# A small load that nothing reads, in front of the first load of a rotary embedding kernel

## The chip, the cores and the metric

The kernel runs on one core of one Trainium2 chip. The metric is the device time of one execution in microseconds (us), the median of several runs. The kernel before takes 316.29 us (three runs, 316.23 to 316.83).

## What is computed

A rotary position embedding with interleaved pairs. `x` has the shape (8, 2048, 16, 64): batch, position, head, head dimension, in fp32. `cos` and `sin` have the shape (2048, 32). The reference, cut to what matters:

```python
x_pairs = x.reshape(batch, seq_len, num_heads, head_dim // 2, 2)
x1, x2 = x_pairs[..., 0], x_pairs[..., 1]
out1 = x1 * cos - x2 * sin
out2 = x1 * sin + x2 * cos
out = np.stack([out1, out2], axis=-1).reshape(batch, seq_len, num_heads, head_dim)
```

`x` is 67.1 MB and so is the output.

## The kernel before

**Tiling.** The 2048 positions of a batch are spread over 128 partitions, 16 rows (`K`) to each. A row is 16 heads of 64 numbers, 1024 fp32 or 4 KB, so one partition's share of a batch is one piece of 64 KB in the DRAM. In SBUF a batch is kept in bf16. The buffer `xt` has five places for a batch; `HOME` gives the place of each of the eight batches, so that batches 5, 6 and 7 come to where 0, 1 and 2 were. GpSimd's DMAs turn fp32 into bf16 on the way in and back on the way out (`load`, L68 to L70, and `store`, L72 to L74).

**The head.** The first 4 rows of batch 0 go another way, so that work can start early: SyncE (SP) loads them in fp32 (L101) into the buffer `head`, which shares its place with the scratch buffer `qt`, and ScalarE (ACT) casts them into `xt` (L108). Meanwhile GpSimd (POOL) issues, on its own queue and in this order: sin (L102), cos (L103), rows 4 to 15 of batch 0 (L104), batches 1 and 2 in one DMA, batches 3 and 4 in one DMA (both L70).

**The work.** VectorE (DVE) makes two tables from sin and cos (L110 to L112) and then calls `rotate` for the 4 rows, the other 12 rows, and each of the seven other batches. A `rotate` is three operations over all its rows: the product with the sin table into `qt` (L89), the product with the cos table in place (L92), and the sum with the pairs of `qt` swapped (L97).

**The order.** It is written out by hand under `tc.manual_schedule()`; each engine works its own queue in the order of the lines, and waits between engines are put in where data are shared. The store of batch 0 is held back until DVE has come to batch 2, by two tiny copies on ACT (L120, L121). A tiny copy on POOL that reads the end of batch 4 (`mark`, L126) stands ahead of the store of batches 1 and 2. Batches 5, then 6 and 7, are loaded when the places that they come to have been stored. The last batch leaves in another way: ACT casts it to fp32 in four parts into places 3 and 4 of `xt` (`wide`, L138), and SP stores it (L139). SP has only these two DMAs, L101 and L139.

**Buffers.** The pool `consts` holds `xt`, the tables, and the two single numbers `gate` and `mark`; the pool `stage` behind it holds the one buffer that `head` and `qt` share.

Of the kernel before, what the change touches and what calls it, by code (L numbers as in the profile page):

```python
# [2 lines left out]

# [4 lines left out]


@with_exitstack  # L10
def kernel(
    ctx: ExitStack,
    tc: tile.TileContext,
    x: bass.AP,
    cos: bass.AP,
    sin: bass.AP,
    out: bass.AP,
):
    nc = tc.nc
    fp32 = mybir.dt.float32  # L20
    bf16 = mybir.dt.bfloat16
    mult = mybir.AluOpType.mult
    add = mybir.AluOpType.add

    B, S, H, D = x.shape
    P = 128
    K = S // P
    KP = 16
    D2 = D // 2
    HD = H * D  # L30
    NX = 5
    HEAD = 4
    PART = 4
    STAGE = 3


    HOME = [0, 1, 2, 3, 4, 0, 1, 2]

    x_t = x.rearrange("b (p k) h d -> b p k (h d)", p=P, k=K)
    out_t = out.rearrange("b (p k) h d -> b p k (h d)", p=P, k=K)  # L40
    x_r = x.rearrange("b (p k) h d -> p b (k h d)", p=P, k=K)
    out_r = out.rearrange("b (p k) h d -> p b (k h d)", p=P, k=K)
    cos_t = cos.rearrange("(p k) c -> p (k c)", p=P, k=K)
    sin_t = sin.rearrange("(p k) c -> p (k c)", p=P, k=K)

    consts = ctx.enter_context(tc.tile_pool(name="consts", bufs=1))
    stage = ctx.enter_context(tc.tile_pool(name="stage", bufs=1))

    xt = consts.tile([P, NX, K * HD], bf16)
    cos_sb = consts.tile([P, K * D2], fp32)  # L50
    sin_sb = consts.tile([P, K * D2], fp32)
    c_tab = consts.tile([P, K, D], bf16)
    s_tab = consts.tile([P, K, D], bf16)

    wide = (
        xt[:, STAGE : STAGE + 2]
        .rearrange("p a c -> p (a c)")
        .bitcast(fp32)
        .rearrange("p (k c) -> p k c", c=HD)
    )  # L60

    gate = consts.tile([1, 1], bf16)
    mark = consts.tile([1, 1], bf16)

    def home(b, k0=0, k1=K):
        return xt[:, HOME[b], k0 * HD : k1 * HD].rearrange("p (k c) -> p k c", c=HD)

    def load(b, n):  # L68
        h = HOME[b]
        nc.gpsimd.dma_start(out=xt[:, h : h + n], in_=x_r[:, b : b + n])  # L70

    def store(b, n):  # L72
        h = HOME[b]
        nc.gpsimd.dma_start(out=out_r[:, b : b + n], in_=xt[:, h : h + n])  # L74

    def rotate(b, k0=0, k1=K, between=None):
        nk = k1 - k0
        xp = home(b, k0, k1)
        qt = stage.tile([P, KP, HD], bf16, name="qt", tag="work")

        def rows(a):
            return a.rearrange("p k (h e) -> p k h e", h=H, e=D)

        def tab(a):
            return dataclasses.replace(
                a, offset=a.offset + k0 * D, ap=[a.ap[0], [D, nk], [0, H], [1, D]]
            )

        nc.vector.tensor_tensor(out=rows(qt[:, :nk]), in0=rows(xp), in1=tab(s_tab), op=mult)  # L89
        if between is not None:  # L90
            between(qt)
        nc.vector.tensor_tensor(out=rows(xp), in0=rows(xp), in1=tab(c_tab), op=mult)  # L92
        q_swap = dataclasses.replace(
            qt, offset=qt.offset + 1, ap=[qt.ap[0], [2, nk * HD // 2], [-1, 2]]
        )
        x3 = xp.rearrange("p k (a j) -> p (k a) j", j=2)
        nc.vector.tensor_tensor(out=x3, in0=x3, in1=q_swap, op=add)  # L97

    with tc.manual_schedule():
        head = stage.tile([P, HEAD, HD], fp32, name="st", tag="work")  # L100
        nc.sync.dma_start(out=head[:, :HEAD], in_=x_t[0, :, :HEAD])  # L101
        nc.gpsimd.dma_start(out=sin_sb, in_=sin_t)  # L102
        nc.gpsimd.dma_start(out=cos_sb, in_=cos_t)  # L103
        nc.gpsimd.dma_start(out=home(0, HEAD), in_=x_t[0, :, HEAD:])  # L104
        load(1, 2)
        load(3, 2)

        nc.scalar.copy(out=home(0, 0, HEAD), in_=head[:, :HEAD])  # L108
        s2 = s_tab.rearrange("p k (i j) -> p (k i) j", j=2)
        nc.vector.tensor_copy(out=s2[:, :, 0], in_=sin_sb)  # L110
        nc.vector.tensor_scalar_mul(s2[:, :, 1], sin_sb, -1.0)  # L111
        nc.vector.tensor_copy(  # L112
            out=c_tab.rearrange("p k (i j) -> p (k i) j", j=2),
            in_=cos_sb.to_broadcast([P, K * D2, 2]),
        )
        rotate(0, 0, HEAD)
        rotate(0, HEAD, K)

        def first_store(qt):
            nc.scalar.copy(out=gate, in_=qt[:1, KP - 1, HD - 1 :])  # L120
            nc.scalar.copy(out=xt[:1, HOME[0], :1], in_=xt[:1, HOME[0], :1])  # L121
            store(0, 1)

        rotate(1)
        rotate(2, between=first_store)
        nc.gpsimd.tensor_copy(out=mark, in_=xt[:1, 4, K * HD - 1 :])  # L126
        store(1, 2)
        load(5, 1)
        load(6, 2)
        rotate(3)  # L130
        rotate(4)
        store(3, 2)
        for b in range(5, B):
            rotate(b)
            if b == 6:
                store(5, 2)
        for k in range(0, K, PART):
            nc.scalar.copy(out=wide[:, k : k + PART], in_=home(B - 1, k, k + PART))  # L138
        nc.sync.dma_start(out=out_t[B - 1], in_=wide)  # L139


# [1 line left out]
_INS = ['x', 'cos', 'sin']  # L143
_OUTS = [((8, 2048, 16, 64), 'float32')]


# [23 lines left out]
```

## Time and profile before

| what | value |
|---|---|
| time, median of three runs | 316.29 us (316.23 to 316.83) |
| time of the profiled execution | 316.21 us |
| span of the profiled execution, first to last instruction | 314.4 us |
| DVE busy | 210.4 us, 67% of the span, 30 instructions |
| ACT busy, POOL busy | 19.3 us (6%), 12.4 us (4%) |
| DMA queue q0, issued by POOL | 91.75 MB, counted as written, 92.0% of 16 engines' span |
| DMA queue q1, issued by SP | 10.49 MB, counted as written, 7.9% |
| head (L101): 2048 KB, from issue to landing | 8.0 us |
| sin (L102), cos (L103): 256 KB each | 7.6 and 7.4 us |
| rows 4 to 15 of batch 0 (L104): 3072 KB in bf16 | 21.2 us |

The span runs from the first to the last instruction of the profile; the profiled execution's own time holds 1.8 us more around it. A line such as `L101 SPq` is an instruction by which SP's queue issues a DMA: its length is the time of the issue, not of the transfer. The busy share of the DMA is the mean over the core's 16 DMA engines, on which all queues run. A DMA is cut into packets, which the trace records one by one with their starts, lengths and sizes.

### The profile page before, as it was taken

To read this page: it belongs to the slowest core of one execution; us is meant where nothing else is said; L and a number is where in the kernel's file an instruction comes from. 1 tells how busy PE (TensorE), PEld (TensorE's weight loads), DVE (VectorE), ACT (ScalarE), POOL (GpSimd) and SP (SyncE) were. 2 spreads that over 40 slices of the span, in tenths; PEclk is the share of its full clock that TensorE was granted. 3 is DMA by queue.
4 is the path that set the end of the run, shared out by engine and by line. 5 is a ranking of instruction groups with operands and counts; after the bars stand their busy time and mean duration, and the time that the engine had idled before them with its cause. 6 is when DMAs were issued, how large, how long until landed. Compare 5 with 4: busy or idle time off the path is not lost.

```text
span 314.4 us, 114 instructions
## 1 busy us (share of the span) xinstructions
DVE 210.4 (67%) x30; ACT 19.3 (6%) x8; POOL 12.4 (4%) x16
## 2 busy tenths in 40 slices
DVE  0549950099999999999992299903999999200000
ACT  1400000000000000000000000000000000790000
POOL 4000000000002500000000000000000000000000
DMA  7999999999999999999999999999999999999996
GB/s 296 238 267 200 200 200 267 200 200 217 250 200 267 459 475 400 400 492 442 400 200 246 221 200 200 250 217 333 400 525 409 400 400 525 409 400 400 525 409 267
DMA packets 2512, 102.24 MB, mean 325 GB/s; under 512 B 208, under 2 KB 208, under 8 KB 336
## 3 DMA queue, kind: packets, MB, share of 16 engines
q0 software_dynamic: 2224, 91.75, 92.0%
q1 hardware_dynamic: 288, 10.49, 7.9%
HBM read 67.63 MB, written 67.11 MB: 429 GB/s over the span
## 4 chain that ended last, share of the span: by engine, by line
DVE 64%; another core or an unknown queue 13%; DMA 7%; ACT 3%; ACTq 1%; issue 0%; POOL 0%; DVEq 0%; PEldq 0%
DVE qt L89 21%; DVE xt L92 21%; DVE xt L97 21%; DMA xt<-in_x_dram 7%; ACT xt L138 3%; ACTq L165 1%; POOL sin_sb L102 0%; POOL cos_sb L103 0%; DVEq L89 0%; DVEq L92 0%; PEldq L165 0%
## 5 line engine op out<-in xcount | busy, mean ns | idle before, releaser
L89 DVE TENSOR_TENSOR qt<-xt,s_tab 128x16384 bf16<-128x16384 bf16 (+2 forms) x9 | 69.7, 7744 | 49.3 <-DMA xt<-in_x_dram 47.0
L92 DVE TENSOR_TENSOR xt<-xt,c_tab 128x16384 bf16<-128x16384 bf16 (+2 forms) x9 | 69.7, 7743 | 0.4
L97 DVE TENSOR_TENSOR xt<-xt,qt 128x16384 bf16<-128x16384 bf16 (+2 forms) x9 | 69.7, 7744 | 0.3
L138 ACT CAST xt<-xt 128x4096 f32<-128x4096 bf16 x4 | 14.1, 3600 | 171.7 <-DVE xt L97 171.7
L74 POOL DMA_DIRECT2D out_dram<-xt x4 | 2.7, 672 | 184.9 <-ACT xt L121 93.5
L110 DVE CAST s_tab<-sin_sb 128x512 bf16<-128x512 f32 x1 | 0.5, 456 | 8.9 <-DMA sin_sb<-in_sin_dram 8.9
L120 ACT COPY gate<-qt 1x1 bf16<-1x1 bf16 x1 | 0.2, 194 | 85.1 <-DVE qt L89 85.1
L126 POOL COPY mark<-xt 1x1 bf16<-1x1 bf16 x1 | 5.0, 5040 | 2.6 <-DMA xt<-in_x_dram 2.6
L70 POOL DMA_DIRECT2D xt<-in_x_dram x4 | 2.7, 694 | 43.2 <-DMA out_dram<-xt 43.2
L108 ACT CAST xt<-st 128x4096 bf16<-128x4096 f32 x1 | 3.6, 3605 | 6.7 <-DMA st<-in_x_dram 6.7
L108 ACT ACT_TABLE_LOAD x1 | 1.3, 1283 | 0.7 <-PEq L154 0.7
L102 POOL DMA_DIRECT2D sin_sb<-in_sin_dram x1 | 0.7, 696 | 0.8 <-PEq L165 0.8
L112 DVE CAST c_tab<-cos_sb 128x1024 bf16<-128x1024 f32 x1 | 0.7, 685 | 0.0
L103 POOL DMA_DIRECT2D cos_sb<-in_cos_dram x1 | 0.6, 569 | 0.0
L104 POOL DMA_DIRECT2D xt<-in_x_dram x1 | 0.6, 557 | 0.0
L111 DVE TENSOR_SCALAR s_tab<-sin_sb 128x512 bf16<-128x512 f32 x1 | 0.4, 445 | 0.0
L121 ACT COPY xt<-xt 1x1 bf16<-1x1 bf16 x1 | 0.2, 188 | 0.0
L154 POOL MEMSET const-float32-0.0<- 128x1 f32 x1 | 0.1, 99 | 0.2 <-issue 0.2
L154 POOL MEMSET const-bfloat16-1.0<- 128x1 bf16 x1 | 0.1, 103 | 0.0
L154 POOL MEMSET const-float32-1.0<- 128x1 f32 x1 | 0.1, 99 | 0.0
L154 POOL MEMSET const-uint8-127<- 128x1 uint8 x1 | 0.1, 99 | 0.0
## 6 DMA issues: line engine op xcount, KB each, us to landing
xt<-in_x_dram POOLq DMA_DIRECT2D x3, 8192.0 KB, 59.4
xt<-in_x_dram POOLq DMA_DIRECT2D x1, 4096.0 KB, 57.6
xt<-in_x_dram POOLq DMA_DIRECT2D x1, 3072.0 KB, 21.2
st<-in_x_dram SPq DMA_DIRECT2D x1, 2048.0 KB, 8.0
sin_sb<-in_sin_dram POOLq DMA_DIRECT2D x1, 256.0 KB, 7.6
cos_sb<-in_cos_dram POOLq DMA_DIRECT2D x1, 256.0 KB, 7.4
out_dram<-xt POOLq DMA_DIRECT2D x4, 49.8
out_dram<-xt SPq DMA_DIRECT2D x1, 30.0
```

The costliest lines, as they stand in the source:

```text
L70: nc.gpsimd.dma_start(out=xt[:, h : h + n], in_=x_r[:, b : b + n])
L74: nc.gpsimd.dma_start(out=out_r[:, b : b + n], in_=xt[:, h : h + n])
L89: nc.vector.tensor_tensor(out=rows(qt[:, :nk]), in0=rows(xp), in1=tab(s_tab), op=mult)
L92: nc.vector.tensor_tensor(out=rows(xp), in0=rows(xp), in1=tab(c_tab), op=mult)
L97: nc.vector.tensor_tensor(out=x3, in0=x3, in1=q_swap, op=add)
L102: nc.gpsimd.dma_start(out=sin_sb, in_=sin_t)
L103: nc.gpsimd.dma_start(out=cos_sb, in_=cos_t)
L108: nc.scalar.copy(out=home(0, 0, HEAD), in_=head[:, :HEAD])
L112: nc.vector.tensor_copy(out=c_tab.rearrange("p k (i j) -> p (k i) j", j=2), in_=cos_sb.to_broadcast([P, K * D2, 2]),)
L126: nc.gpsimd.tensor_copy(out=mark, in_=xt[:1, 4, K * HD - 1 :])
L138: nc.scalar.copy(out=wide[:, k : k + PART], in_=home(B - 1, k, k + PART))
L165: with _tile.TileContext(nc) as tc:
```

## The change

A buffer of 32 partitions by 128 fp32 is added to `consts`, behind `gate` and `mark`. Ahead of the head's load, SP loads into it the first 128 numbers (512 bytes) of the first row of every fourth partition's share of batch 0: 32 pieces of 512 bytes, 16 KB, 256 KB apart in the DRAM. These bytes are part of what the head's load reads, too. Nothing reads the buffer.

```diff
     gate = consts.tile([1, 1], bf16)
     mark = consts.tile([1, 1], bf16)
+    touch = consts.tile([32, 128], fp32)
...
     with tc.manual_schedule():
         head = stage.tile([P, HEAD, HD], fp32, name="st", tag="work")
+        nc.sync.dma_start(out=touch, in_=x_t[0, ::4, 0, :128])
         nc.sync.dma_start(out=head[:, :HEAD], in_=x_t[0, :, :HEAD])
         nc.gpsimd.dma_start(out=sin_sb, in_=sin_t)
         nc.gpsimd.dma_start(out=cos_sb, in_=cos_t)
```

## The prediction

> **What bounds the kernel now.** I read four views in this order: the page's forty slices, the windows, the start of the timeline, and the costs by DMA issue. The page first, since no engine that computes is near full (DVE 67%):
>
> ```profile
> DMA  7999999999999999999999999999999999999996
> ...
> q0 software_dynamic: 2224, 91.75, 92.0%
> q1 hardware_dynamic: 288, 10.49, 7.9%
> HBM read 67.63 MB, written 67.11 MB: 429 GB/s over the span
> ```
>
> Each digit is the busy share of the 16 DMA engines. It is 7 in the first slice, 6 in the last, 9 in the 38 between. Slice by slice the DVE row falls to 2 or 0 while this row never does. The two queues together are busy for 99.9% of 16 engines' span; packets that overlap are counted twice, so 99.9 is a little too high, but it leaves no room for a pause. The windows say the same in stretches (time, then DVE, ACT, POOL, clock, and DMA share and GB/s last):
>
> ```profile
> 0.00:0.74 0.74, 0.00 (x0) 0.01 (x1) 0.20 (x4) 1.00 0.00 0
> 0.74:1.74 1.00, 0.00 (x0) 1.00 (x1) 0.47 (x1) 1.00 0.00 0
> 1.74:2.00 0.26, 0.00 (x0) 0.26 (x1) 0.26 (x2) 1.00 3.54 819
> ...
> 60.00:100.00 40.00, 37.33 (x5) 0.29 (x2) 0.56 (x1) 1.00 0.97 210
> 100.00:140.00 40.00, 39.81 (x5) 0.00 (x0) 6.32 (x3) 1.00 1.04 446
> ...
> 313.20:314.40 1.20, 0.00 (x0) 0.00 (x0) 0.00 (x0) 1.00 0.00 0
> ```
>
> A packet is booked where it starts, hence 3.54 in the stretch in which all of them start. From 1.75 us on, the DMA engines never rest until 313.2 us. So the chain of waits, which names DVE for 64% of the span, names the wrong bound: DVE's work lies in the shadow of a queue that is always full, and where DVE waits (18.9 us ahead of 62.5 us, 11 and 12 us later) it waits for that queue. I counted it once more on the trace's records of single packets: between 1.75 and 5 us the places that are empty, out of 16, add up to 0.22 us, and from 5 to 311.5 us there are never fewer than 16 packets in flight. The time of this kernel is therefore: when the DMA engines start (1.75 us) + the work put on them (311.5 us) + the end (1.2 us in the span and 1.8 us outside it: 316.21 minus 314.4).
>
> What ends at 1.75 us? The timeline (start, length, engine, line):
>
> ```profile
> 0.74 0.38 SPq L101 DMA_DIRECT2D st<-in_x_dram  x1
> 1.27 0.70 POOL L102 DMA_DIRECT2D sin_sb<-in_sin_dram  x1 [0.82 <-PEq L165]
> 1.96 0.57 POOL L103 DMA_DIRECT2D cos_sb<-in_cos_dram  x1
> ```
>
> SP starts to issue the head at 0.74 and its first packet starts at 1.75, 1.01 us later. GpSimd's first packet (sin) starts at 5.46 by the packet records, 4.2 us after its issue. So for 3.7 us the head is the only thing that the engines can do, and whatever delays the head leaves them idle.
>
> **The change part by part.** It removes nothing and adds one buffer, one issue on SP ahead of the head, and 16 KB of reading.
>
> *The issue.* The head's issue is moved behind one more DMA instruction of the same queue. SP's two DMA instructions took 378 ns (L101) and 348 ns (L139). The new one has 32 rows in place of 128; if its cost went with the rows it would be a quarter, 95 ns. Both rows at hand move 128 partitions, with pieces four times apart (16 KB and 64 KB), and differ by 8% alone, so I take the 378 ns and keep 95 as the low end. Nothing else stands on SP's queue before 283.5 us. GpSimd does not wait for SP, so L102 to L104 and L70 issue when they did. The head's first packets go from 1.75 to 2.13 us. As the engines have nothing else before 5.46 us, all later packets move by that: **+0.38 us** (0.10 at the low end).
>
> *The bytes.* 32 rows of 512 bytes over 16 engines are 1 KB for each. The head's packets of 16 KB took 0.61 us each from the third round on, 26.9 bytes per ns, so 1 KB is 0.04 us. It would be moved between 1.75 and 2.13 us, when the engines are idle: **0**, or +0.04 if that cover is gone.
>
> *The first packets.* The first packet of each of the 16 engines took 1.10 us on average, the second round 0.64, later ones 0.61: 0.49 us is lost once. What for, no view shows, and the two ends follow from it. If it is a price of the first access, the small load pays it from 1.75 us on, beside the wait for the head's issue, and the head is relieved of up to 0.49 us. If it is the way of any packet through empty engines, or 16 engines in step at the memory, the head pays it as before: 0. The nearest other row is the first round of sin's packets, the first access of its queue to a tensor not touched before: 0.176 us against a mean of 0.161 for all 128 packets of sin and cos, on engines that are already running. A new region and a new queue cost 0.015 us there. That speaks against a price of the first access, so I take **0**, and keep -0.49 as the end.
>
> *In order behind the small load.* Two rows per engine stand in the ring ahead of the head. If an engine starts the head while they are under way, nothing is added. If it finished each before the next, two packets with 0.49 us of empty way and 0.02 us of moving would be 1.02 us, from 1.75 to 2.77 us, in place of 2.13. In the running stream 16 KB packets follow each other in 0.61 us without 0.49 between them, so packets are not done one by one there: **0**, with +0.64 (2.77 less 2.13) as the end. By the Trainium skill (DMA: Bandwidth & Descriptors, section Latency and other measured facts) a tiny transfer has a least round trip of about 800 ns whatever its size; a head that had to wait for one such trip would start at about 2.55 us, an estimate from that page, and the sum would be +0.8. The same page (section Two DMAs through the same engine are not ordered) says that descriptors start in order but are pipelined, by which the sum stays at +0.38; the steady packets above agree, but no row here shows a small load alone on idle engines.
>
> *The buffer.* 512 bytes per partition behind `mark` push the stage buffer up. Nothing waits for `touch`, and it stands under nobody's write. A slower DVE, if the new address made one, is covered: the stores stand in the queue before the engines are free for them. L74's first was issued at 98.0 us for a transfer that can't start before the load ahead of it lands at 101; the SP store at 283.5, while store(5, 2) still had its bytes to move. The cover is thinnest at 101 (3 us), and the landing that starts DVE's run to it, at 62.4, shifts by as much as the stream, so the cover stays. **0.** The end of the kernel waits for one more semaphore, long full: the waits for semaphores listed in the trace take about 0.02 to 0.05 us each. **0**, at most +0.05.
>
> *The head's readers.* ACT's cast L108 starts at 8.74, when the head is there, DVE's first rotation follows and ends at 19.3; then DVE waits 4.5 us for rows 4 to 15 (23.8 us). 0.38 us later is hidden by that 4.5; what is late next is the load of rows 4 to 15 itself, by the same 0.38 us.
>
> **Sum.** 316.21 (the profiled execution) + 0.38 = 316.59, so 316.6. The median of the runs, 316.29, is 0.08 higher and would give 316.67. A measurement of this kernel can tell about 0.2% from no change, 0.63 us; the forecast is 0.12%: within.
>
> **The rivals.**
> - *Warmed* (chance 0.24): the small load takes over the dear first round. +0.38 - 0.49 = -0.11: 316.1. For it: early first packets lasted longest in time when 16 started together, and by 3.3 us all of them were over, about when a delayed head would begin to profit. Against it: sin's first round.
> - *Stopped behind* (0.18): the engines work the small rows off one at a time before the head: +0.38 + 0.64 = +1.02: 317.2, slower by 0.3%. Place: the rings, 1.75 to 2.8 us. It decides for slower once the head's first packet starts later than about 2.4 us (1.75 + 0.63). For it: 1.10 us for a first packet shows how long an empty way is. Against it: the steady stream.
> - *Not ahead* (0.07): the load that nothing reads is not issued in front of the head, or its issue is as cheap as its rows: 0 to +0.10, 316.2 to 316.3.
> - *Early all round* (0.04): besides the 0.49 us, the late start of the last engines goes too (its first packet starts at 2.46, their mean is 1.93, a loss of 0.53): 0.38 - 0.49 - 0.53 = -0.64: 315.6.
>
> **How the numbers follow.** The forecast, a plain shift, has 0.47, of which I put 0.03 beyond 0.63 us for the spread of the runs (316.23 to 316.83). Slower by over 0.2%: 0.18 + 0.03 = 0.21, less 0.01 for a stop that is short: 0.20. Faster by over 0.2%: 0.04, and 0.01 of *warmed* with a low run: 0.05. Within: 0.75. The range takes in *warmed* at 316.1 with 0.1 for scatter, and the middle of *stopped behind* at 317.2: 316.0 to 317.2; left out are *early all round* and the upper half of *stopped behind*, 0.13.
>
> **What would show it.** In the profile after: two SPq issues, the head's about 0.38 us later (near 1.1 us); the head's main packets from about 2.1 us; the landing of the head near 9.1 in place of 8.7, of rows 4 to 15 near 24.1, DVE's start on batch 1 near 62.9, and a span of 314.8. *Warmed* shows the head issued later but landing as before; *stopped behind* shows DVE's start on batch 1 over 0.6 us late. I am wrong in kind, not in size, if the DMA row shows a pause anywhere after 3 us, or if packets of the later loads take other than the present time, 2.43 us each in the loads of two batches.

## The result, and the profile after

The kernel with the small load takes 316.69 us (median of 22 runs, 316.58 to 317.44), the kernel before 316.27 us (22 runs beside it, 316.01 to 317.03). The ratio is 1.0014 with a 95% interval of 1.0007 to 1.0020. That is 0.42 us more, 0.13%; the forecast was +0.38. The interval does not reach down to 1, so the kernel with the small load is slower, by less than 0.2%.

The start of the timeline of the changed kernel (start, length, engine, line; the lines of the code have moved by one or two):

```profile
0.74 0.38 SPq L102 DMA_DIRECT2D touch<-in_x_dram  x1
1.18 0.41 SPq L103 DMA_DIRECT2D st<-in_x_dram  x1
1.27 0.69 POOL L104 DMA_DIRECT2D sin_sb<-in_sin_dram  x1 [0.83 <-PEq L167]
...
9.17 3.61 ACT L110 CAST xt<-st 128x4096 bf16<-128x4096 f32 x1 [7.15 <-DMA st<-in_x_dram]
...
24.27 6.56 DVE L90 TENSOR_TENSOR qt<-xt,s_tab 128x12288 bf16<-128x12288 bf16 x1 [4.52 <-DMA xt<-in_x_dram]
```

The same two readers of the loads in the kernel before:

```profile
8.74 3.60 ACT L108 CAST xt<-st 128x4096 bf16<-128x4096 f32 x1 [6.73 <-DMA st<-in_x_dram]
...
23.84 6.56 DVE L89 TENSOR_TENSOR qt<-xt,s_tab 128x12288 bf16<-128x12288 bf16 x1 [4.52 <-DMA xt<-in_x_dram]
```

SP now issues twice, and the head's issue stands at 1.18 in place of 0.74 us: 0.38 for the instruction and 0.06 to the next. GpSimd's issue of sin has not moved. ACT's cast starts at 9.17 (8.74 before), DVE's first operation on rows 4 to 15 at 24.27 (23.84 before), and DVE's wait for that load is 4.52 us in both. So what follows the head is 0.43 us late up to here; DVE's start on batch 1 is 0.37 us late (62.90 in place of 62.53) and the last packet 0.42. Nothing is stretched.

The windows of the same execution, at the start (DMA share and GB/s last):

```profile
0.74:1.74 1.00, 0.00 (x0) 1.00 (x1) 0.47 (x1) 1.00 0.00 0
1.74:2.20 0.46, 0.00 (x0) 0.28 (x1) 0.46 (x2) 1.00 0.13 36
2.20:4.20 2.00, 0.00 (x0) 0.00 (x0) 2.00 (x4) 1.00 1.07 328
```

In the 0.46 us in which the kernel before starts 14 of the head's 16 first packets, the engines are now busy for 13% and move 36 GB/s: that is the small load. The rest of it is the idle time which the change costs. Later slices of the page read as before:

```profile
DMA  7999999999999999999999999999999999999996
...
q0 software_dynamic: 2224, 91.75, 91.9%
q1 hardware_dynamic: 336, 10.50, 8.0%
```

And the costs by DMA issue (KB each, us from issue to landing):

```profile
st<-in_x_dram SPq DMA_DIRECT2D x1, 2048.0 KB, 8.0
sin_sb<-in_sin_dram POOLq DMA_DIRECT2D x1, 256.0 KB, 8.1
...
touch<-in_x_dram SPq DMA_DIRECT2D x1, 16.0 KB, 1.7
```

The head still takes 8.0 us from its issue, so it is not relieved by the small load and not held up by it. Sin takes 8.1 us where it took 7.6, with the same issue: its first packet starts at 5.85 us (5.46 before), when 80 of the head's 128 packets have started.

### The profile page after: what moved, and what is told of

Read it like the earlier page. It is cut to its first block, busy times and chain, and to the rows that moved or that the text cites. A ratio compares the mean times of both kernels' runs of the same rounds, so it can differ in the third digit from the quotient of the medians.

```text
span 314.9 us, 115 instructions
## 1 busy us (share of the span) xinstructions
DVE 210.4 (67%) x30; ACT 19.3 (6%) x8; POOL 12.3 (4%) x16
## 4 chain that ended last, share of the span: by engine, by line
DVE 64%; another core or an unknown queue 13%; DMA 7%; ACT 3%; ACTq 1%; issue 0%; POOL 0%; DVEq 0%; PEldq 0%
DVE qt L90 21%; DVE xt L93 21%; DVE xt L98 21%; DMA xt<-in_x_dram 7%; ACT xt L140 3%; ACTq L167 1%; POOL sin_sb L104 0%; POOL cos_sb L105 0%; DVEq L90 0%; DVEq L93 0%; PEldq L167 0%
```

## The experiments

The theory: the DMA engines are the bound from their first packet to the last, so the cost is the useful work by which they are behind after the start, and here that is the time by which SP issues the head later. Rivals: the extra DMA costs by itself wherever it stands (its buffer, its semaphore, its bytes); the small load holds the head up on the engines; a price is paid once by whatever is first.

To compare the starts, I summed for each profiled execution the packets moved by 10 us, each counted at its steady time (16 KB of the head: 0.611 us) and the small loads left out, over 16 engines. "Behind" is what is missing against the kernel before; "last packet" is the shift of the last packet's end in the same two executions; "runs" is the difference of the medians.

| kernel | head issued at, us | behind at 10 us | last packet | runs |
|---|---|---|---|---|
| the change | 1.18 | 0.48 | +0.42 | +0.42 |
| small load behind the head | 0.74 | 0.61 | +0.54 | -0.04 |
| small load on ACT's queue | 0.74 | 0.01 | -0.03 | +0.10 |
| two small loads | 1.63 | 0.84 | +0.91 | +0.89 |
| four | 2.56 | 1.61 | +3.23 | +3.26 |
| six | 3.48 | 1.93 | +4.28 | +4.02 |
| eight | 4.45 | 2.89 | +16.57 | +16.56 |
| 512 KB in front | 1.16 | 1.41 | +1.48 | +1.45 |
| head as rows 0, then 1 to 3 | 0.74, 1.16 | 0.47 | +0.60 | +0.58 |
| head as rows 0 to 2, then 3 | 0.74, 1.17 | 0.32 | +0.36 | +0.26 |
| sin from SP, then the head | 1.15 | 0.36 | +0.37 | +0.26 |

Where "last packet" and "runs" differ, the profiled execution was not a middle one; the last section says what the executions differ in. The ratios given below are worked out over all runs and are not the quotients of the two medians: for sin from SP, the ratio is 1.0002 beside a difference of the medians of 0.26 us.

### The small load behind the head

```diff
-        nc.sync.dma_start(out=touch, in_=x_t[0, ::4, 0, :128])
         nc.sync.dma_start(out=head[:, :HEAD], in_=x_t[0, :, :HEAD])
+        nc.sync.dma_start(out=touch, in_=x_t[0, ::4, 0, :128])
```

> The same small load, buffer and semaphore, issued by SP right behind the head's load instead of in front. Theory (idle engines: the cost is the time by which the head's first packet is late, nothing else): the head's packets start at 1.75 us again, the 16 KB lie inside the full stream and cost 0.04 us; ratio to the kernel before 1.0001, span 314.4 to 314.5, DVE's start on batch 1 at 62.5 to 62.6. Rival (the cost lies in the extra DMA itself, its buffer, its semaphore or its wait at the end, wherever it stands): ratio 1.0014, span 314.9.

Measured: 316.22 us against 316.26, ratio 1.0000 (0.9991 to 1.0009). The head's issue is in front again:

```profile
0.74 0.36 SPq L102 DMA_DIRECT2D st<-in_x_dram  x1
1.16 0.42 SPq L103 DMA_DIRECT2D touch<-in_x_dram  x1
```

Buffer, bytes and semaphore are all there, and the cost is gone: the rival falls. The profiled execution itself took 316.74 us and a span of 315.0, not the 314.4 expected; the middle of the 11 runs has 314.4.

### The small load on ACT's queue

```diff
-        nc.sync.dma_start(out=touch, in_=x_t[0, ::4, 0, :128])
+        nc.scalar.dma_start(out=touch, in_=x_t[0, ::4, 0, :128])
```

> The same small load, issued by ACT on its own queue in place of SP. Theory: SP issues the head at 0.74 us again, the engines start on it at 1.75 us, ratio 1.0001, span 314.4 to 314.5; ACT's cast waits for the head until 8.7 us, so ACT's issue of about 0.4 us is hidden. Rival (what delays the head is not SP's issue but the small load standing ahead on the 16 engines, or one descriptor generator that SP and ACT share): the head's first packet still near 2.2 us, span 314.8 to 314.9.

Measured: 316.36 us against 316.26, ratio 1.0004 (0.9995 to 1.0012). The timeline of this kernel:

```profile
0.74 0.40 ACTq L102 DMA_DIRECT2D touch<-in_x_dram  x1
0.74 0.37 SPq L103 DMA_DIRECT2D st<-in_x_dram  x1
1.17 1.28 ACT L110 ACT_TABLE_LOAD   x1 [1.17 <-PEq L156]
```

Both issues run at once, the head's first packet is at 1.75 us again, and the span is 314.4. The 0.43 us by which ACT's table load is late lie in ACT's wait for the head. It is SP's queue that the change pays with. The interval alone would not exclude +0.0012; the trace of the start does. One part of the rival this kernel does not test: the small load's packets did not stand ahead of the head here, the first of them started at 2.62 us, behind the head's first packets. That part is read from the change itself, where they did: the head's first packet came 1.03 us after its issue there (1.18 to 2.21), and 1.01 us in the kernel before.

### Two small loads in front

```diff
-        nc.sync.dma_start(out=touch, in_=x_t[0, ::4, 0, :128])
+        for i in range(2):
+            nc.sync.dma_start(out=touch[:, i], in_=x_t[0, ::4, i, :128])
```

> Two small loads of 16 KB in front of the head on SP, of rows 0 and 1, into two parts of one buffer. Theory: each issue ahead moves the head's issue by another 0.44 us (0.74, 1.18, 1.62), the head's first packet to about 2.66 us, the time by 0.85 us over before: ratio 1.0027, span 315.3. Rival (a cost that is paid once, by the first small load): as with one, ratio 1.0014, span 314.9.

Measured: 317.15 us, ratio 1.0024 (1.0014 to 1.0034), span 315.3. The start of the timeline:

```profile
0.74 0.84 SPq L103 DMA_DIRECT2D touch<-in_x_dram  x2
1.27 0.70 POOL L105 DMA_DIRECT2D sin_sb<-in_sin_dram  x1 [0.83 <-PEq L168]
1.63 0.42 SPq L104 DMA_DIRECT2D st<-in_x_dram  x1
```

The second load costs again; a cost paid once would have left 1.0014, which is the low end of the interval, but the head's issue at 1.63 us and the last packet at +0.91 decide it. The packet records show one thing more: GpSimd's first packet now starts at 2.67 us, not at 5.46 or 5.85, although its issue is where it was. Twelve of sin's packets start ahead of the head's first, which comes at 3.11 us and not at the 2.66 of the theory. So with two loads the idle time already ends with sin's packets, not with the head's: 2.67 less 1.75 is 0.92 us, and that the theory's 0.85 came so near is in part luck. In the kernels with the head's issue at 1.63 us or later GpSimd's first packet starts at 2.67 to 2.69 us, in all others at 5.40 us or later. I read this as sin's packets standing behind the head on the engines, where they could have come from 2.67 us on; what holds them back there, no run shows. ACT's small packets, in the experiment above, did get in between the head's from 2.62 us on.

### Eight

The same edit with 8.

> Eight small loads of 16 KB in front of the head on SP. If nothing else can start: head issued at 0.74 + 8 x 0.44 = 4.26 us, first packet at 5.3, time +3.5 us: ratio 1.011, span 317.9. Theory, as the profile after suggests it (sin's first packet moved by 0.39 us with the head although its issue stayed at 1.27 us, so it stood behind the head's packets and was not late by itself): GpSimd's packets come onto idle engines well before 5.3 us and the engines work on sin, cos and batch 0 while the head is on its way; the cost then stops growing at the time of GpSimd's first packet less 1.75 us. GpSimd's issue of sin is over at 1.97 us; with 1.0 us to a first packet, as SP needs, that is about 3.0 us, so about +1.2 us: ratio 1.004, span 315.6. The head lands near 11 us in place of 8.7, inside the 4.5 us for which DVE waits later.

Measured: 332.82 us, ratio 1.0516 (1.0501 to 1.0530). Both forecasts are far off. The timeline of this kernel:

```profile
0.74 3.67 SPq L103 DMA_DIRECT2D touch<-in_x_dram  x8
...
4.45 1.04 SPq L104 DMA_DIRECT2D st<-in_x_dram  x1
...
50.21 3.60 ACT L111 CAST xt<-st 128x4096 bf16<-128x4096 f32 x1 [48.19 <-DMA st<-in_x_dram]
53.85 2.29 DVE L90 TENSOR_TENSOR qt<-xt,s_tab 128x4096 bf16<-128x4096 bf16 x1 [47.99 <-ACT xt L111]
```

The head, issued 3.7 us later, lands 41 us later. GpSimd's packets came first, and from there the engines take packets of the two queues in turn: in the records the eight rounds of the head's packets lie 3.03 us apart, which is one packet of batches 1 and 2 (2.43 us) and one of the head (0.61). They begin at 23.2 us, behind the small loads, which alternated with batch 0 in the same way. The Trainium skill (DMA: Bandwidth & Descriptors, section Queues, rings and completion order) says that an engine goes round robin between the queues it has work for, packet by packet. The 3.03 us here, against 2.43 + 0.61 = 3.04, agree. The turns are not taken from the start on, though: in the kernel before, 82 of the head's 128 packets had started before sin's first at 5.46 us. DVE so starts 41 us late and becomes the bound, as its windows show (DMA share and GB/s last):

```profile
100.00:104.00 4.00, 4.00 (x1) 0.00 (x0) 0.00 (x0) 1.00 0.73 156
104.00:116.00 12.00, 11.93 (x3) 0.28 (x2) 0.00 (x0) 1.00 0.00 0
```

All loads have landed, and there is nothing to store before DVE is through with its first operation on batch 2 at 115.5 us: the engines rest. By the packet records they rest for 13.6 us there, and with the 2.9 us from the start that is 16.5 of the 16.57.

### Four and six

The same edit with 4 and with 6.

> Four small loads in front of the head. Theory, as eight and two have shaped it: the cost of the late start is capped where GpSimd's first packet comes onto idle engines, 2.69 us, so 2.69 less 1.75, about 0.9 us; past that the head competes with GpSimd's packets one for one. The head stands where the fifth small load of eight stood (packets from about 4.6 us), its 8 packets per engine alternate with those of batch 0 (1.83 + 0.61 us a pair), so it lands near 24 us in place of 8.7; DVE has 26.6 us of work from there to batch 1 and is through by about 55, before batches 1 and 2 land at 63. So time +0.9 to +1.3 us, ratio 1.003 to 1.004. Rival (the cost grows in proportion, eight having cost 16.5 us): half of that, +8 us, ratio 1.026.

> Six small loads in front of the head. Theory: the head stands where the seventh of eight stood, packets from about 15.7 us, 2 more pairs with packets of batch 0 (2.44 us) and 6 with those of batches 1 and 2 (2.43 + 0.61 us): landing near 39 us. DVE then needs 3.6 us of cast and 26.6 us of its own work: batch 1 begins near 69 us, 6 us later than the load would allow, of which the store of batch 0 hides 3 to 4; time +3 to +4 us, ratio 1.009 to 1.013. Rival (in proportion to eight): +12 us, ratio 1.039.

Measured: four 319.49 us, ratio 1.0095 (1.0080 to 1.0109); six 320.25 us, ratio 1.0113 (1.0095 to 1.0131). Six agrees in size, four took 2 to 2.4 us more than the theory. The rival of growth in proportion falls in both. For four, the head landed near 27 us (forecast: near 24), as the timeline shows:

```profile
2.56 0.42 SPq L104 DMA_DIRECT2D st<-in_x_dram  x1
...
27.09 3.60 ACT L111 CAST xt<-st 128x4096 bf16<-128x4096 f32 x1 [25.07 <-DMA st<-in_x_dram]
...
65.79 8.69 DVE L90 TENSOR_TENSOR qt<-xt,s_tab 128x16384 bf16<-128x16384 bf16 x1 [8.35 <-DMA xt<-in_x_dram]
```

DVE was in time for batch 1 and waited 8.35 us for it; the load was late. Three terms make 3.1 of the 3.23 us in the packet records: 1.61 behind at 10 us (the cap of 0.9 did not hold, as the engines rested for 1.2 us in the mean between 1.75 and 10 us, where they rested for 0.2 in the kernel before, and first packets were dear again), 0.48 of idle engines near 102 us, where the store of batch 0 was issued at 101.28 when DVE had come so far, and about 1.0 in which the engines no longer end together. For six the same terms are 1.93, 1.03 and 1.10, 4.1 of the 4.28 us. The head landed near 35 us there (forecast: near 39), and batch 1 began at 66.8 us, released by its load and not by DVE, so six was right in size by another sum than mine, by luck.

### 512 KB in front

```diff
-    touch = consts.tile([32, 128], fp32)
+    touch = consts.tile([P, HD], fp32)
...
-        nc.sync.dma_start(out=touch, in_=x_t[0, ::4, 0, :128])
+        nc.sync.dma_start(out=touch, in_=x_t[0, :, 0])
```

> One load in front of the head as in the change, but of 128 rows of 4 KB: 512 KB, 1.22 us of work for 16 engines by the rate of the head's steady packets. Theory (idle engines): the bytes are moved from 1.75 us on while the head's issue is under way, so cost is the larger of the two, 1.2 us, not their sum; ratio 1.0039. Rival (issue and bytes add): 0.42 + 1.22 = 1.64 us, ratio 1.0052.

Measured: 317.68 us, ratio 1.0043 (1.0031 to 1.0055). It is +1.45, between the larger of the two (1.22) and their sum (1.64), and the interval holds both. The trace decides against the sum: the head's packets start at 3.55 us with no pause before them. The 512 KB took 2.04 us of each engine in place of 1.27 at the steady time, and in turn the head's first round, at 0.615 us, was not dear any more. So the dear start moved from the head to the load in front of it. The numbers agree: the 2.04 us in front, less the 0.55 us that the head's own packets no longer lose, leave 1.49 us, and the last packet moved by 1.48.

### The head in two loads

```diff
-        nc.sync.dma_start(out=head[:, :HEAD], in_=x_t[0, :, :HEAD])
+        nc.sync.dma_start(out=head[:, :1], in_=x_t[0, :, :1])
+        nc.sync.dma_start(out=head[:, 1:HEAD], in_=x_t[0, :, 1:HEAD])
```

and in a second kernel with `:3` and `3:HEAD`.

> No small load; the head itself goes in two DMAs of SP, row 0 (512 KB) and then rows 1 to 3. Theory: the second issue is as late as the head is in the change (1.18 us), but the engines have 1.2 us of useful work from 1.75 us on, so nothing is lost: ratio 1.000, span 314.4. Rival (a second DMA on SP's queue ahead of the bulk of the head costs its 0.42 us whatever it moves): ratio 1.0013, span 314.9.

> The head in two DMAs of SP again, but rows 0 to 2 first (1.5 MB, 3.7 us of work) and row 3 behind. The split of 1 + 3 rows cost 0.5 us although no engine was idle: its 4 KB packets were dear at the start (0.62 us each in the first round where 0.16 is the steady time, in sum 0.62 us per engine over the row) and again at the seam of the two DMAs (0.2 to 0.3). If the dear start with small packets does it, nothing is lost with 12 KB packets first: ratio 1.000 to 1.0006. Rival (a second SP DMA costs its issue of 0.42 us): ratio 1.0013. Second rival (the seam does it): ratio about 1.001, with slow packets where the row 3 follows.

Measured: 1 + 3 rows 316.81 us, ratio 1.0015 (1.0007 to 1.0024); 3 + 1 rows 316.57 us, ratio 1.0009 (1.0000 to 1.0018). My theory said 1.000 for the first and is missed. The rival, that it costs an issue, hits the number of the first but not the way: the first packets start at 1.75 us in both. In 3 + 1 the second issue is covered by 3 us of work, and the packets at the seam took their steady 0.159 us, so the seam is out there. What is dear is the start. Packets over their steady time cost each engine 0.80 us in the head of 1 + 3 and 0.13 in sin and cos, 0.84 in the pieces of 12 KB of 3 + 1, and 0.59 in the head of the kernel before. Why smaller pieces start worse is left open.

### Sin from SP, ahead of the head

```diff
-        nc.sync.dma_start(out=head[:, :HEAD], in_=x_t[0, :, :HEAD])
-        nc.gpsimd.dma_start(out=sin_sb, in_=sin_t)
+        nc.sync.dma_start(out=sin_sb, in_=sin_t)
+        nc.sync.dma_start(out=head[:, :HEAD], in_=x_t[0, :, :HEAD])
```

> Without the small load; SP issues sin's load (256 KB, in one piece in the DRAM, 0.6 us of work) ahead of the head, and GpSimd no longer issues it. The head's issue is as late as in the change, but the engines have useful work in the meantime. Theory (idle engines): ratio 1.000, with up to 0.0006 more if sin's packets of 2 KB are dear at the start as the split's were. Rival (whatever stands in front of the head costs its issue): ratio 1.0014.

Measured: 316.57 us against 316.31, ratio 1.0002 (0.9993 to 1.0011). The head's issue is at 1.15 us, as late as in the change. The interval takes in no cost, and seven of the eleven runs (316.13 to 316.82) lie below the lowest of the 22 runs of the change, 316.58: a late head costs less if what stands in front is work that has to be done anyway. That it is free is not shown, as the interval reaches up to 0.35 us and the medians differ by 0.26. The profiled execution, 316.57, was 0.36 us behind after its start, with its first packet at 1.73 us: sin's packets lost 0.38 us per engine against their steady time, and the head's still lost 0.65 behind them (0.59 in the kernel before). So sin's 256 KB did not take the dear start from the head, as the 512 KB did.

None of the ten is faster than the kernel before.

## Why the prediction was right, point by point

- *The bound.* It held. Wherever the loads alone were disturbed, the last packet moved by what was missing at 10 us, within 0.13 us. The chain of waits named DVE for 64% in both kernels. With four, six and eight small loads DVE did bound a stretch between 100 and 117 us, where the engines rested for 0.48, 1.03 and 13.6 us. In the changed kernel they do not rest between 3 and 311.5 us, and the packets of the loads of two batches take 2.43 us as before, so neither sign of being wrong in kind came.
- *The issue, +0.38.* Measured +0.44 from issue to issue (0.38 and a step of 0.06 that I left out), +0.46 for the head's first packet, +0.42 for the last packet and for the runs. 32 rows cost SP what 128 rows cost, 0.38 us; the low end of 0.10 was wrong.
- *The reason for it was in part wrong.* I took 5.46 us for the time at which GpSimd can first serve the engines. With two small loads it is 2.67. So the idle time can grow one for one with the delay only up to about 0.9 us. At 0.44 this changed nothing.
- *The bytes, 0.* Right: the 32 packets took 0.026 us each, between 1.75 and 2.16 us.
- *The first packets, 0.* Right: the head's first round took 1.15 us after the small load, 1.10 before. *Warmed* falls. (Over all eight rounds the head's packets lost 0.66 us per engine, 0.59 before; the prediction counted 0.49, the first round alone.) But 512 KB in front did relieve the head, so it is no property of an empty way either: a first packet of 512 bytes took 0.026 us.
- *Early all round* did not come, and was priced too high: its 0.53 us is the last engine's first start less the mean (2.46 less 1.93). What 16 engines lose by starting unevenly is the mean less the first start, 0.18 us, and it is 0.18 in the changed kernel, too.
- *In order behind the small load, 0.* Right: the head's first packet starts at 2.214 us, 0.06 after the small load's last record at 2.15 and 1.03 after its own issue (1.01 before). *Stopped behind* falls for one small load. The small load landed 1.7 us after its issue, at 2.44 us, and the head did not wait for that. The least round trip that the Trainium skill gives (DMA: Bandwidth & Descriptors, section Latency and other measured facts) so did not come into the sum. What the same page of the Trainium skill says of pipelined descriptors (section Two DMAs through the same engine are not ordered) agrees: the head's first packets started before the small load had landed.
- *The buffer and the semaphore, 0.* Right, by the kernel that has both and the order reversed.
- *The head's readers.* Forecast 9.1, 24.1, 62.9 and a span of 314.8; measured 9.17, 24.27, 62.90 and 314.9.

## What to carry to other kernels

First read whether the DMA engines ever rest. If they do not, the first load's issue is on the critical path for its full time, as long as no other queue has work for the engines yet. Then even a very small load put in front of it costs one issue (0.44 us here); on another idle queue it cost nothing that could be told. A dummy load did not pay: 16 KB did not make the next load's packets cheaper, and 512 KB did but cost more than that. Where two queues share the engines, it matters who comes first: here the 2 MB that everything waits for, issued behind another queue's bulk, got one packet in turn with that bulk's longer ones, and 3.7 us of delay became 41.

## What the runs showed that was not expected

- The scatter of the runs (316.0 to 317.0 for one kernel) can arise in the first packets. In the profiled execution of the kernel with the small load behind the head (316.74 us, where the median is 316.22), the head's first round took 1.64 us in place of 1.10; its packets lost 0.55 us more per engine than before's, and the last packet ended 0.54 us later. The later packets of GpSimd's queue took the same times in both (2.432 us in the loads of two batches, 2.447 in the stores).
- The packets on engines that have just begun to move data are dear: against their steady times they lost 0.59 us per engine in the kernel before, 0.8 to 1.0 with the 512 KB in front, with the split heads and with sin from SP, and 1.14 in the execution just named. A load of 16 KB does not pay this; one of 512 KB pays it in the head's place; sin's 256 KB paid 0.38, and the head behind it paid again. What causes it no run here tells.
- The cost of a late head is a cliff, not a line: 0.42, 0.89, 3.3, 4.0 and 16.6 us for one, two, four, six and eight small loads, which issue the head 0.44, 0.89, 1.82, 2.74 and 3.71 us later.
